# Moving SBUF tiles by 64 bytes: which half of each 128-byte line a matmul's two operands start in

## The chip, the cores and the metric

The program runs on one core of a Trainium2 chip. The metric is the device time of one execution in microseconds, 2118.91 before (median of 3 runs, 2118.55 to 2119.3). Five engines work side by side: TensorE (PE, which multiplies, with PEld as its weight loads), VectorE (DVE), ScalarE (ACT), GpSimd (POOL) and SyncE (SP, which issues most transfers). PE reads a *moving* operand (its columns stream through the array) and *weights* (a 128x128 block that a LDWEIGHTS instruction puts into the array) from SBUF, the on-chip memory, and writes PSUM.

## The reference

A two-layer encoder over 512 tokens of width 1024, float32 throughout. Per layer:

```python
h = h + 0.5 * swiglu(rmsnorm(h, g), wg, wu, wd)        # first feed-forward part, width 2816
h = h + mixer(rmsnorm(h, mix_g), ...)                  # attention; layer 0 and layer 1 differ
h = h + memory_xattn(rmsnorm(h, mg), rmsnorm(mem, sg), ...)   # attention to 256 memory rows
h = h + 0.5 * swiglu(rmsnorm(h, g), wg, wu, wd)        # second feed-forward part
# swiglu(x) = (silu(x @ wg) * (x @ wu)) @ wd
```

So there are four feed-forward parts, two mixers and two memory attentions, one after the other.

## The kernel before, in words

Activations lie transposed: eight tiles `x` of 128 features x 512 tokens. Every float32 product is done as three products of float32r parts: a tile is split into a high part (`xh`, `wh`, `hh`, a copy by ACT) and a low part (`xl`, `wl`, `hl`, what is left, by DVE), and high x high, low x high and high x low are added in PSUM.

**A feed-forward part** (`ffn`) first does one pair of 128-column blocks of gate and up with ordinary 512-column matmuls (`plain_pair`, L319). The other ten pairs are done by a scheme with seven products of half-size operands in place of eight (`open_pair`, `sum_pair`, `cross_pair`, `close_pair`). Each such product (`product`, L446) is 24 matmuls of 256 moving columns: two halves z, three pairs of parts, four blocks k. The moving operand is a quarter of the activations, either half of the tiles `xh`/`xl` or one of four combinations made once per part (`t1h`/`t1l` to `t4h`/`t4l`). The weights are a 128x1024 quarter or a sum or difference of quarters, split by `operand` into `wh`/`wl` (L424 on ACT, L425 on DVE); every third product has its split tiles `sh`/`sl` in a second pool of the feed-forward part instead. 4 parts x 10 pairs x 7 products make 280 products, 6720 matmuls. After enough pairs, `down` multiplies the hidden tiles `hh`/`hl` by the down weights in 512-column matmuls (L581), three times per part: 8, 8 and 6 hidden blocks deep, eight output blocks each.

**A mixer** weaves its projections (L683, the weights `wh`/`wl` moving, 512 columns, `xh`/`xl` as the loaded weights) with attention (L789, L814, L841, L897), the memory projection (`mem_kv`, L1080) and the output projection (`out_proj`, L634); memory attention follows (L1172 to L1230).

**Order.** PE's order is the order of the code. The order of the other engines is made at build time by a scheduler from dependencies and a cost model that knows no addresses. Places in SBUF are given by pools: a pool takes a stretch of each partition, and a tile's rotating buffers (`bufs`) lie behind one another in it, in the order in which tags first appear. Two pieces of padding in the pools `const` and `small` (PAD_CONST, PAD_SMALL, in float32) decide where what follows begins.

Of the kernel before, what the change touches and what calls it, by code (L numbers as in the profile page):

```python
# [11 lines left out]
F32 = mybir.dt.float32  # L12
F32R = mybir.dt.float32r
# [6 lines left out]
P = 128  # L20
# [39 lines left out]
WS = (2, 3, 0, 1, 1, 2, 1, 2, 0, 0, 3, 2, 1, 1, 0, 3)  # L60
FIRST = (0, 1, -1, 2, 3, -2, 4, 5, 6, -3, -4, 7)

PAD_CONST = 24
PAD_SMALL = 80

LEAD, REST = ((0, 0), (0, 1)), ((1, 0),)

# [39 lines left out]
class Encoder:  # L107
    def __init__(self, tc, ctx, I):
# [14 lines left out]
        nc.vector.memset(self.ones, 1.0)  # L123
        self.mhalf = self.const.tile([P, 8 + PAD_CONST], F32, name="mhalf")
        nc.vector.memset(self.mhalf, -0.5)
# [18 lines left out]
        return self.bank("pa" if self.pflip else "pb")  # L144

    def wtile(self):
        return [self.wp.tile([P, 1024], dt, name=n, tag=n, bufs=b) for n, dt, b in (("wf", F32, 3), ("wh", F32R, 2), ("wl", F32R, 2))]

    def behind(self, ins):

# [265 lines left out]
    def operand(self, t, own=None):  # L416

        nc, f = self.nc, self.f
        if own is None:
            own = f.n % 3 == 2  # L420
            f.n += 1
        h, l = [(f.tp if own else self.wp).tile([P, 1024], F32R, name=n, tag=n, bufs=1 if own else 2)
                for n in (("sh", "sl") if own else ("wh", "wl"))]
        self.leading = nc.scalar.activation(h, t, AF.Copy)  # L424
        self.parted = nc.vector.tensor_sub(l, t, h.bitcast(F32))  # L425
        return h, l
# [133 lines left out]
    def block(self, c, d, own=False):  # L560

        nc, f = self.nc, self.f
        n = CHUNKS[c] * P
        src = self.I[f.pre + "wd"][d, :, sum(CHUNKS[:c]) * P:sum(CHUNKS[:c]) * P + n]
        if not own:
            return self.wload(src, n), self.bank2()
        with self.tc.high_priority():
            w = self.wp.tile([P, 1024], F32, name="wf", tag="wf", bufs=3)
            h, l = [f.tp.tile([P, 1024], F32R, name=t, tag=t, bufs=1) for t in ("sh", "sl")]
            self.wfill((w, h, l), src, slice(0, n), nc.vector)  # L570
        return (h, l), self.bank2()

    def down_products(self, c, block, ops, tail):

        f = self.f
        (w, bank), nb = block, CHUNKS[c]
        for a, e in ops:
            for j in range(nb - 2, nb) if tail else range(nb - 2):
                b = sum(CHUNKS[:c]) + j
                h = f.H[b // 2][e][:, b % 2 * S:b % 2 * S + S]  # L580
                self.nc.tensor.matmul(bank, w[a][:, j * P:(j + 1) * P], h, start=j == a == e == 0,  # L581
                                      stop=j == nb - 1 and (a, e) == ops[-1])
# [420 lines left out]
    def index_keys(self, out, p, epsv, r, mp):  # L1003
# [23 lines left out]
        nc.vector.scalar_tensor_tensor(r2, r, (64 ** -0.5) * (8 ** -0.5), r, op0=OP.mult, op1=OP.mult)  # L1027
        coef = self.small.tile([P, 32 + PAD_SMALL], F32, name="coef", tag="coef", bufs=1)[:, :32]
        nc.vector.tensor_mul(coef.rearrange("p (i h) -> p i h", h=8), n3[:, :, 64:72],
# [526 lines left out]
```

## Time and profile before

| what | value |
|---|---|
| median of the runs | 2118.91 us |
| profiled execution, first to last instruction (its span) | 2114.9 us |
| PE busy in it | 2082.3 us, 98% |
| PEld busy | 1853.8 us, 88% |
| DVE busy | 1571.9 us, 74% |
| ACT busy | 1136.0 us, 54% |
| mean granted TensorE clock | 0.998 |

The profiled execution's own time is known as its span only; the median of the runs stands 4.0 us above it (what lies ahead of the first and behind the last instruction). A matmul's busy time of 280 or 390 ns overlaps that of the next, so busy times of PE don't say how fast matmuls follow one another; their starts do. The list of instructions in order of time gives these: a row is a run of like matmuls with the start of its first, so the difference of two rows' starts over the number of matmuls between is the pitch.

### The profile page before, as it was taken

Reading aid. Unit: us, or ns where it says so; the run is one execution under the profiler, and the core shown is the slowest. Engines: PE = TensorE matmul, PEld = TensorE weight load, DVE = VectorE, ACT = ScalarE, POOL = GpSimd, SP = SyncE. Lnnn points to the kernel's source line nnn. Section 1 sums busy time; section 2 is a strip of 40 time slices with the busy share of each in tenths; the row PEclk is TensorE's granted clock in tenths of the full one; section 3 lists DMA queues with packets and bytes.
Section 4 is the critical chain, followed back from the end, with each engine's and each line's share of the span. In section 5 each row is a group of like instructions: output and inputs, shape, how many; then the busy total and the mean of one; then the engine's idle time right before and its main releaser. Section 6 shows DMA issues by size and latency. Waiting matters only on the chain.

```text
span 2114.9 us, 32522 instructions
## 1 busy us (share of the span) xinstructions
PE 2082.3 (98%) x12834; PEld 1853.8 (88%) x12834; DVE 1571.9 (74%) x2246; ACT 1136.0 (54%) x1701; POOL 364.4 (17%) x319
## 2 busy tenths in 40 slices
PE   8999999999999999999999999999999999999999
PEld 7989898877788889898989899988888888989897
DVE  8858677579876697685789677684668688958676
ACT  6636344466686565362556354354678566626442
POOL 1111003345431120000020000013453122000000
PEclk9999999999999999999999999999999999999999
DMA  7836535222241266474356466334223225736532
GB/s 231 211 119 181 150 93 180 87 75 70 82 133 63 68 188 171 132 190 127 98 167 175 130 170 178 99 119 153 81 89 125 96 70 149 190 110 189 160 98 93
DMA packets 86121, 279.65 MB, mean 132 GB/s; under 512 B 9680, under 2 KB 12880, under 8 KB 85968
## 3 DMA queue, kind: packets, MB, share of 16 engines
q1 hardware_dynamic: 74448, 235.62, 33.5%
q0 software_dynamic: 11520, 41.95, 11.1%
q8 instruction: 101, 1.65, 0.3%
q14 instruction: 52, 0.43, 0.1%
HBM read 271.24 MB, written 6.29 MB: 131 GB/s over the span
## 4 chain that ended last, share of the span: by engine, by line
PE 90%; DVE 6%; ACT 2%; issue 1%; DMA 0%; POOL 0%; SPq 0%; DVEq 0%; POOLq 0%; ACTq 0%
PE ps_pa L446 26%; PE ps_pa L683 11%; PE ps_pa L581 11%; PE ps_pb L581 11%; PE ps_pb L446 10%; PE ps_pa L634 4%; PE ps_pa L319 3%; PE ps_pb L789 2%; PE ps_pa L1230 2%; PE ps_pb L841 1%; PE ps_pa L1080 1%; PE ps_pb L634 1%; PE ps_pb L814 1%; PE ps_pa L999 1%; PE ps_pb L319 1%
## 5 line engine op out<-in xcount | busy, mean ns | idle before, releaser
L157 ACT ACTIVATE wh<-wf 128x1024 fp32r<-128x1024 f32 (+2 forms) x211 | 215.5, 1022 | 353.2 <-PE ps_pa L581 119.4
L159 DVE TENSOR_TENSOR wl<-wf,wh 128x1024 fp32r<-128x1024 f32 (+2 forms) x169 | 200.3, 1188 | 49.9 <-ACT wh L157 48.0
L424 ACT ACTIVATE wh<-s 128x1024 fp32r<-128x1024 f32 x108 | 114.4, 1059 | 108.8 <-PE ps_pb L446 34.8
L425 DVE TENSOR_TENSOR wl<-s,wh 128x1024 fp32r<-128x1024 f32 x108 | 132.7, 1228 | 51.3 <-ACT wh L424 49.5
L424 ACT ACTIVATE wh<-wf 128x1024 fp32r<-128x1024 f32 x84 | 88.9, 1058 | 110.1 <-PE ps_pa L446 36.0
L503 POOL DMA_DIRECT2D s<-l_ffn_wq x40 | 35.5, 887 | 538.7 <-ACT s L502 517.0
L159 POOL TENSOR_TENSOR wl<-wf,wh 128x1024 fp32r<-128x1024 f32 x42 | 102.2, 2433 | 141.1 <-ACT wh L157 139.5
L683 PE MATMUL ps_pa<-wh,xh 128*128 128x512 f32 x384 | 123.6, 403 | 0.0
L683 PE MATMUL ps_pa<-wh,xl 128*128 128x512 f32 x384 | 120.2, 394 | 0.0
L683 PE MATMUL ps_pa<-wl,xh 128*128 128x512 f32 x384 | 119.5, 393 | 0.0
L476 POOL DMA_DIRECT2D s<-l_ffn_wq x40 | 35.6, 889 | 442.3 <-DMA s<-l_ffn_wq 314.8
L425 DVE TENSOR_TENSOR wl<-wf,wh 128x1024 fp32r<-128x1024 f32 x84 | 102.7, 1222 | 9.4 <-ACT wh L424 6.5
L591 DVE TENSOR_TENSOR dn<-ps_pa,R 128x512 f32<-128x512 f32 x48 | 33.1, 689 | 89.2 <-PE ps_pa L581 88.9
L581 PE MATMUL ps_pb<-hh,wl 128*128 128x512 f32 x352 | 96.6, 393 | 0.0
L581 PE MATMUL ps_pb<-hl,wh 128*128 128x512 f32 x352 | 96.5, 392 | 0.0
L581 PE MATMUL ps_pb<-hh,wh 128*128 128x512 f32 x352 | 96.4, 392 | 0.0
L224 POOL TENSOR_TENSOR acc<-acc,sq 128x512 f32<-128x512 f32 (+1 forms) x37 | 52.4, 1416 | 248.2 <-ACT sq L223 247.0
L581 PE MATMUL ps_pa<-hh,wl 128*128 128x512 f32 x328 | 89.7, 392 | 0.0
L581 PE MATMUL ps_pa<-hl,wh 128*128 128x512 f32 x328 | 89.5, 392 | 0.0
L581 PE MATMUL ps_pa<-hh,wh 128*128 128x512 f32 x328 | 89.5, 392 | 0.0
L591 DVE TENSOR_TENSOR dn<-ps_pb,R 128x512 f32<-128x512 f32 x48 | 33.1, 689 | 73.3 <-PE ps_pb L581 72.8
L683 PEld LDWEIGHTS ps_pa<-wh,xl 128*128 128x128 f32 x384 | 73.1, 190 | 16.2
(377 smaller groups left out, 5949.4 us busy)
## 6 DMA issues: line engine op xcount, KB each, us to landing
wf<-l_ffn_wq SPq DMA_DIRECT2D x120, 512.0 KB, 3.5
s<-l_ffn_wq SPq DMA_DIRECT2D x80, 512.0 KB, 4.6
s<-l_ffn_wq POOLq DMA_DIRECT2D x80, 512.0 KB, 6.5
wf<-l_ffn_wd SPq DMA_DIRECT2D x64, 512.0 KB, 3.7
wf<-l_w_in SPq DMA_DIRECT2D x48, 512.0 KB, 3.2
wf<-l_ffn_wd SPq DMA_DIRECT2D x32, 384.0 KB, 3.1
wf<-l_mem_wkv SPq DMA_DIRECT2D x16, 512.0 KB, 3.2
wf<-l_w_out SPq DMA_DIRECT2D x16, 512.0 KB, 3.2
```

Of the source, the lines that this page charges most:

```text
L157: self.leading = nc.scalar.activation(wh[:, sl], w[:, sl], AF.Copy)
L159: eng.tensor_sub(wl[:, sl], w[:, sl], wh.bitcast(F32)[:, sl])
L224: self.summed = (eng or nc.gpsimd).tensor_add(acc[:, :n], acc[:, :n], sq[:, :n])
L319: nc.tensor.matmul(p, w[a][:, k * P:(k + 1) * P], xs[k][c], start=k == order[0] and a == c == 0, stop=k == order[-1] and a == 1)
L424: self.leading = nc.scalar.activation(h, t, AF.Copy)
L425: self.parted = nc.vector.tensor_sub(l, t, h.bitcast(F32))
L446: self.nc.tensor.matmul(bank[:, sl], w[a][:, o:o + P], xs[k][b], start=first and z == a == b == k == 0, stop=z == a == 1 and k == KB // 2 - 1,
L581: self.nc.tensor.matmul(bank, w[a][:, j * P:(j + 1) * P], h, start=j == a == e == 0, stop=j == nb - 1 and (a, e) == ops[-1])
L591: nc.vector.tensor_mul(t, bank, f.R)
L634: nc.tensor.matmul(banks[dd], a[:, o:o + P], parts(k)[b], start=k == first and a is wh and b == 0, stop=k == last and a is wl)
L683: nc.tensor.matmul(banks[i], xs[k][a][:, i * P:(i + 1) * P], w[b][:, kk * 512:kk * 512 + 512], start=k == a == b == 0, stop=k == KB - 1 an ...
L789: nc.tensor.matmul(bank[:, o:o + n], a, b[:, :n], start=c == 0, stop=c == len(ops) - 1)
```

## The change

It moves tiles in SBUF by multiples of 64 bytes. An address bit is meant by its value: bit 6 is worth 64 bytes. All blocks that a matmul takes out of one tile begin at multiples of 512 bytes from the tile's start, so bit 6 is one for a whole tile.

- PAD_CONST and PAD_SMALL go from 24 to 40 and from 80 to 64 floats: 64 bytes more ahead, as many less behind.
- The tiles `wh`, `wl` and `sh`, `sl` get 32 floats (128 bytes) more room, so that the 1024 columns in use can begin 0 or 16 floats into them.
- `operand`, which splits the weights of the seven-product scheme, begins its columns 16 floats in (bit 6 clear), but for every sixth product (LOCK) at 0 (bit 6 set). Other users of the tiles begin at 0.

In the two programs as built, the places of the operands of the matmuls are these, in bit 6 as (moving, weights):

| matmuls | number | before | after |
|---|---|---|---|
| seven-product scheme, 256 columns | 280 products of 24 | 84 (0,0), 52 (1,1), 36 (0,1), 108 (1,0) | 236 (1,0), 44 (1,1) |
| down products, 512 columns | 2112 | 2040 (1,0), 72 (1,1) | all (1,1) |
| plain pairs, projections, queries, index, output, 512 columns | 2424 | (0,0) | (1,1) |
| memory projection, 512 columns | 192 | (0,1) | (1,1) |
| attention products in float32r | 688 | (1,1) | (1,1) |

No instruction is added, removed or moved on any engine: the two programs have the same rows in the same order with the same waits. One memset of a padded constant (`mhalf`) writes 48 in place of 32 columns.

```diff
-PAD_CONST = 24
-PAD_SMALL = 80
+PAD_CONST = 40
+PAD_SMALL = 64
+
+LINE = 16
+WIDE = 1024 + 2 * LINE
+LOCK = 6
@@ wtile
-        return [self.wp.tile([P, 1024], dt, name=n, tag=n, bufs=b) for n, dt, b in (("wf", F32, 3), ("wh", F32R, 2), ("wl", F32R, 2))]
+        return [self.wp.tile([P, c], dt, name=n, tag=n, bufs=b)
+                for n, dt, c, b in (("wf", F32, 1024, 3), ("wh", F32R, WIDE, 2), ("wl", F32R, WIDE, 2))]
@@ operand
-        h, l = [(f.tp if own else self.wp).tile([P, 1024], F32R, name=n, tag=n, bufs=1 if own else 2)
+        o = 0 if f.n % LOCK == LOCK - 1 else LINE
+        h, l = [(f.tp if own else self.wp).tile([P, WIDE], F32R, name=n, tag=n, bufs=1 if own else 2)[:, o:o + 1024]
                 for n in (("sh", "sl") if own else ("wh", "wl"))]
@@ block
-            h, l = [f.tp.tile([P, 1024], F32R, name=t, tag=t, bufs=1) for t in ("sh", "sl")]
+            h, l = [f.tp.tile([P, WIDE], F32R, name=t, tag=t, bufs=1) for t in ("sh", "sl")]
```

## The prediction

> **What bounds the kernel now.** I read the page's busy times, then the chain of work that ended last, then windows of the seven-product matmuls alone, then the list of PE's instructions in order of time. Page:
>
> ```profile
> PE 2082.3 (98%) x12834; PEld 1853.8 (88%) x12834; DVE 1571.9 (74%) x2246; ACT 1136.0 (54%) x1701; POOL 364.4 (17%) x319
> ...
> PE 90%; DVE 6%; ACT 2%; issue 1%; DMA 0%; POOL 0%; SPq 0%; DVEq 0%; POOLq 0%; ACTq 0%
> ```
>
> PE is busy nearly throughout and carries 90% of the chain, so the time moves with PE's pitch. Stretches of the seven-product scheme, L446 alone, and their sum:
>
> ```profile
> 30.00:331.00 301.00, 199.44 (x1680) 198.37 (x1680) 1.00 0.54 149
> ...
> sum 1211.00, PE 796.57 PEld 793.32; mean PE 199.14 PEld 198.33
> ```
>
> The 6720 matmuls take 796.57 us, 2.845 for each of 280 products. How long one product takes depends on its tiles. These are the first rows of ten products that follow each other without a wait (each product has six rows of four matmuls):
>
> ```profile
> 160.15 0.64 PE L446 MATMUL ps_pb<-t1h,sh 128*128 128x256 f32 x4
> ...
> 163.02 0.62 PE L446 MATMUL ps_pa<-t2h,wh 128*128 128x256 f32 x4
> ...
> 163.93 0.62 PE L446 MATMUL ps_pa<-t2h,wl 128*128 128x256 f32 x4
> ...
> 165.74 0.64 PE L446 MATMUL ps_pa<-xh,wh 128*128 128x256 f32 x4
> ...
> 168.62 0.64 PE L446 MATMUL ps_pa<-t3h,sh 128*128 128x256 f32 x4
> ...
> 171.49 0.63 PE L446 MATMUL ps_pa<-xh,wh 128*128 128x256 f32 x4
> ...
> 174.34 0.64 PE L446 MATMUL ps_pa<-t4h,wh 128*128 128x256 f32 x4
> ...
> 177.18 0.63 PE L446 MATMUL ps_pb<-xh,sh 128*128 128x256 f32 x4
> ...
> 179.91 0.62 PE L446 MATMUL ps_pb<-t1h,wh 128*128 128x256 f32 x4
> ...
> 182.63 0.62 PE L446 MATMUL ps_pa<-t2h,wh 128*128 128x256 f32 x4
> ...
> 185.35 0.64 PE L446 MATMUL ps_pa<-xh,sh 128*128 128x256 f32 x4
> ```
>
> Subtract neighbouring starts. In the built program bit 6 is set in the `t` and `sh`/`sl` tiles, clear in `xh`/`xl` and `wh`/`wl`. t1 x sh (1,1), xh x wh (0,0), t3 x sh (1,1), xh x wh (0,0) take 2.87, 2.88, 2.87, 2.85: **equal bits**, 120 ns a matmul. t2 x wh (1,0), xh x sh (0,1), t1 x wh, t2 x wh (1,0) take 2.72, 2.73, 2.72, 2.72: 113.4 ns, the **good** state. t4 x wh at 174.34 takes 2.84 though its bits differ: about 117.8 ns, the **off** state. Counting all 280 products this way I find 136 equal, 75 off, 69 good. 136x2.87 + 75x2.83 + 69x2.72 = 790.3; waits make up the other 6.3 of 796.57. So the trace of before has an effect of the very property that the change sets.
>
> What decides between good and off? In the rows above the (1,0) product after (1,1) is good (163.02), the one after (0,0) off (174.34), and good carries on from product to product (177.18 to 185.35). Over the whole trace, leaving out transitions with a wait: (1,1) to (1,0) gives good 11 times of 11, (0,0) to (1,0) off 35 of 35, good (1,0) to (1,0) stays good 11 of 11, good (1,0) to (0,1) turns off 11 of 11. A wait inside the run can throw it off: after the four transposes near a part's start the scheme is off in all four parts, here 20 matmuls in 2.35 us:
>
> ```profile
> 36.52 0.63 PE L446 MATMUL ps_pb<-t1l,wh 128*128 128x256 f32 x4
> ...
> 38.87 0.64 PE L446 MATMUL ps_pa<-t2h,sh 128*128 128x256 f32 x4
> ```
>
> **The change part by part.** *Instructions:* none is added, removed or moved on any engine, and no wait; only places change. So the sum consists of pitches of PE.
>
> *Seven-product scheme.* 236 products become (1,0), 44 (1,1): per part the products numbered 4, 10, ... 64 of 70. A (1,1) product costs 2.87 and, by 11 of 11, hands over good; then five (1,0) products follow. Bounds: all 236 good, 44x2.87 + 236x2.72 = 768.2, a gain of 22.1 against 790.3; all off, 44x2.87 + 236x2.83 = 794.2, a loss of 3.9. I take 22 off, 5 or 6 a part: products 1 to 3 behind the transposes, the two that follow the early block of the last down call (a wait there), half of product 0; the others lie behind a (1,1) product or behind (1,1) down products, which should hand over alike. 44x2.87 + 22x2.83 + 214x2.72 = 770.7: **19.6 us less**.
>
> *Down products.* 512 columns, (1,0) to (1,1). Rows with equal bits (L319, (0,0), undisturbed, then behind transposes), L581 in an 8-block call, L581 in a last call, and the few L581 with (1,1):
>
> ```profile
> 19.55 1.98 PE L319 MATMUL ps_pa<-xh,wl 128*128 128x512 f32 x8
> ...
> 26.81 0.60 PE L251 MATMUL ps_pb<-ident,acc 128*128 128x128 f32 x4
> 27.16 2.10 PE L319 MATMUL ps_pb<-xh,wh 128*128 128x512 f32 x8
> 29.10 1.99 PE L319 MATMUL ps_pb<-xl,wh 128*128 128x512 f32 x8
> 30.93 1.98 PE L319 MATMUL ps_pb<-xh,wl 128*128 128x512 f32 x8
> 32.74 0.52 PE L446 MATMUL ps_pa<-xh,wh 128*128 128x256 f32 x3
> ```
> ```profile
> 1857.45 1.54 PE L581 MATMUL ps_pa<-hh,wh 128*128 128x512 f32 x6
> ...
> 1865.69 0.62 PE L581 MATMUL ps_pa<-hh,wh 128*128 128x512 f32 x2
> ```
> ```profile
> 1412.97 1.10 PE L581 MATMUL ps_pa<-hh,wh 128*128 128x512 f32 x4
> ...
> 1429.77 0.63 PE L683 MATMUL ps_pa<-wh,xh 128*128 128x512 f32 x2
> ```
> ```profile
> 314.26 1.09 PE L581 MATMUL ps_pa<-hh,sh 128*128 128x512 f32 x4
> ...
> 317.03 0.73 PE L446 MATMUL ps_pb<-xh,wh 128*128 128x256 f32 x4
> ```
>
> Equal bits, settled: 32 matmuls in 7.26 us, 226.9. After a break they need some ten matmuls: 8 in 1.94, 8 in 1.83, 8 in 1.81. L581 (1,0): 36 in 8.24, 228.9, the same in all eight 8-block calls of 192; 72 in 16.80, 233.3, in three of the last calls. L581 (1,1), short: 12 in 2.77, 230.8. So 1536 matmuls from 228.9 to 226.8 give 3.2; some 320 at 233.3 end between 226.9 (2.1) and 230.8 (0.8), I take 1.4 as those runs are broken by waits. **4.6 less**; bounds 5.3 and, all unsettled at 230.8, a loss of 1536x1.9 - 0.8 = 2.1.
>
> *Memory projection.* (0,1) to (1,1), 192 matmuls; the nearest equal group is L683's:
>
> ```profile
> L683 PE MATMUL ps_pa<-wl,xh 128*128 128x512 f32 x384 | 119.5, 393 | 0.0
> ...
> L1080 PE MATMUL ps_pa<-wl,mh 128*128 128x512 f32 x64 | 25.6, 400 | 1.3 <-POOL wl L159 0.8 <-DVE wl L159 0.4
> ```
>
> 7 ns x 192 = 1.3 at most, nothing at least as its runs are short; I take **0.6 less**. The 2424 others go from (0,0) to (1,1), equal both times: nothing.
>
> *Cover.* A faster PE must still be fed. For the product at 163.02 DVE writes `wl` long ahead of its first use at 163.93:
>
> ```profile
> 159.88 1.23 DVE L425 TENSOR_TENSOR wl<-s,wh 128x1024 fp32r<-128x1024 f32 x1 [1.12 <-ACT wh L424]
> ```
> ```profile
> 43.00:331.00 288.00, 287.39 (x2030) 268.39 (x2029) 214.41 (x221) 137.24 (x161) 24.34 (x24) 1.00 0.53 148
> ```
>
> It ends at 161.11, 2.8 us early; five products gain 0.8 at most over the off state, and DVE is busy 214.41 of 288 us in a whole feed-forward stretch. Only the waits in a part's first products grow by what is won just ahead of them, which is next to nothing.
>
> Sum: 19.6 + 4.6 + 0.6 = 24.8. The span of 2114.9 becomes 2090.1; the median of the runs lies 4.0 above the span, so **2094**.
>
> **The rivals.**
>
> *Half good:* the state is lost at boundaries that the trace of before never had, such as good (1,0) to (1,1) and back. With half of the 236 off: 44x2.87 + 118x2.72 + 118x2.83 = 781.2, 9.1 less, with 5.2 from 512 columns 14.3: **2105**. For it: after waits the state was off more often than good. Against: 11 of 11.
>
> *Not bit 6, or not the place at all:* in before, `t` and `sh` lie in an upper region, `x` and `wh` in a lower, so in 256-column products equal bits and equal regions coincide. Were it the region, nothing changes: **2119**. Against: `hh`/`hl` lie partly in the lower region, beside `wh`, with other bit 6, and their eight calls run at 228.9 throughout, never at 226.9. [...]
>
> *All off, 512 columns as forecast:* +3.9 - 5.2: **2117.6**.
>
> *Slower: states are not reached.* Both the good state and the 226.9 are settled ones. If the new boundaries settle in neither, the scheme runs off (+3.9) and the down products at 230.8 (+2.1): +6.0, **2125**. It decides when more than nine tenths of the 236 are off and down stays unsettled; the only row for it is the short (1,1) run at 314.26.
>
> **How the numbers follow.** Forecast 0.73, half good 0.10, not bit 6 or not the place 0.08, all off 0.05, not reached 0.04. A measurement of this kernel can tell about 0.2%, 4.2 us, from no change. Faster: 0.83; same: 0.08 + 0.05 = 0.13; slower 0.04. The forecast's own range is from 2088 (all 236 good, 5.3 and 1.3: 28.7 less, 2090, and a little for a state not seen) to 2102; with the half-good case the range is 2088 to 2107, which leaves out about 2 in 10.
>
> [...]
>
> **What would show it.** L446's counterpart sums to about 777 us in its windows; products start 2.72 apart in fives behind one of 2.87; the down products' rows start 226.9 ns a matmul apart, as L319's do; L683 and waits stay. Wrong would be: fives of 2.83 (handing over fails), products still at 2.87 (not bit 6), new waits of PE on `wl` (DVE became the bound).

## The result, and the profile after

| | before | after |
|---|---|---|
| median of the runs | 2118.73 us (2118.44 to 2119.3, 4 runs) | 2106.93 us (2106.63 to 2109.09, 4 runs) |
| span of the profiled execution | 2114.9 us | 2107.3 us |
| mean granted TensorE clock | 0.998 | 0.997 |

The 2118.91 of the table ahead of the prediction is the median of the first three of these four runs. The ratio is 0.995, 95% interval 0.9935 to 0.9964: faster, by 11.8 us in the medians where 24.8 were forecast. 2106.93 lies at the upper edge of the range of 2088 to 2107. The gain of the seven-product scheme came as forecast; more than half of it was given back, in the 512-column matmuls and in new waits.

The changed file is six lines longer ahead of most of the code. L446 of before is L452 now, and so L424/L425 are L430/L431, L502 is L508, L507 is L513, L319 is L324, L581 is L587, L683 is L689, L634 is L640, L1080 is L1086. The kernels `bit7_equal`, `all_equal`, `scale_after_copy` and `copy_on_dve` of the experiments have one line more (L453, L588), and `before_bit7` has one more than before (L320, L447).

The page of after, busy times and the chain that ended last:

```profile
PE 2072.6 (98%) x12834; PEld 1837.0 (87%) x12834; DVE 1567.4 (74%) x2246; ACT 1137.1 (54%) x1701; POOL 367.1 (17%) x319
...
PE 87%; DVE 7%; ACT 3%; issue 1%; DMA 1%; POOL 0%; SPq 0%; ACTq 0%; DVEq 0%; POOLq 0%
```

PE still bounds the kernel, but 3% of the chain left it, for DVE, ACT and DMA. The busy time of the scheme's matmuls (L452) alone, summed over three windows that hold the whole span:

```profile
sum 2119.00, PE 778.98 PEld 774.62; mean PE 259.66 PEld 258.21
```

That answers the 796.57 of before; about 777 was forecast. The first row of each of seven products of after, in order of time (start, busy, engine, line, operation):

```profile
163.95 0.62 PE L452 MATMUL ps_pa<-t2h,wh 128*128 128x256 f32 x4
...
166.67 0.62 PE L452 MATMUL ps_pa<-xh,wh 128*128 128x256 f32 x4
...
169.39 0.62 PE L452 MATMUL ps_pa<-t3h,sh 128*128 128x256 f32 x4
...
172.11 0.62 PE L452 MATMUL ps_pa<-xh,wh 128*128 128x256 f32 x4
...
174.83 0.63 PE L452 MATMUL ps_pa<-t4h,wh 128*128 128x256 f32 x4
...
177.67 0.63 PE L452 MATMUL ps_pb<-xh,sh 128*128 128x256 f32 x4
...
180.41 0.62 PE L452 MATMUL ps_pb<-t1h,wh 128*128 128x256 f32 x4
```

Four products take 2.72 each, xh x wh and t3 x sh among them, which took 2.87 before. The one at 174.83, a sixth product with (1,1), takes 2.84. Now the 512-column matmuls: the first rows of successive blocks of 24 in an 8-block down call, and behind them the plain pair's rows that were shown of before from 27.16 on:

```profile
113.81 1.53 PE L587 MATMUL ps_pa<-hh,wh 128*128 128x512 f32 x6
...
119.26 1.56 PE L587 MATMUL ps_pb<-hh,wh 128*128 128x512 f32 x6
...
124.85 1.53 PE L587 MATMUL ps_pa<-hh,wh 128*128 128x512 f32 x6
...
130.31 1.56 PE L587 MATMUL ps_pb<-hh,wh 128*128 128x512 f32 x6
...
135.90 1.53 PE L587 MATMUL ps_pa<-hh,wh 128*128 128x512 f32 x6
```
```profile
26.98 2.10 PE L324 MATMUL ps_pb<-xh,wh 128*128 128x512 f32 x8
28.92 2.03 PE L324 MATMUL ps_pb<-xl,wh 128*128 128x512 f32 x8
30.79 2.03 PE L324 MATMUL ps_pb<-xh,wl 128*128 128x512 f32 x8
32.66 0.63 PE L452 MATMUL ps_pa<-xh,wh 128*128 128x256 f32 x4
```

The down blocks alternate: 5.45, 5.59, 5.46, 5.59 us for 24, so 227 and 233 ns a matmul in turn. Before they were 228.9 throughout. The plain pair's groups of eight take 1.94, 1.87, 1.87, where they took 1.94, 1.83, 1.81. Every other block uses the second of the two buffers of `wh`/`wl`. The 128 bytes that the change adds to each of these tiles put the second buffer 4224 bytes behind the first in place of 4096. 4224 is 33 times 128, so bit 7 of the address (worth 128 bytes) is now different in the second buffers. The change was described, and predicted, by bit 6 alone.

The following account adds up the starts of all matmuls in the profiled executions: the sum of the pitches of a group, and apart from it, as wait, what a pitch has above the group's usual one (where it is over 130 ns at 256 columns, 260 at 512).

| us | before | after | bit7_equal | scale_after_copy |
|---|---|---|---|---|
| scheme, pitches (6720) | 790.4 | 771.1 | 774.5 | 765.5 |
| scheme, waits | 5.3 | 10.5 | 8.2 | 5.0 |
| down products (2111) | 484.7 | 486.4 | 479.2 | 479.2 |
| projections L683 (1152) | 263.4 | 265.6 | 263.2 | 263.2 |
| output projection L634 (576) | 131.8 | 132.8 | 131.6 | 131.7 |
| plain pairs L319 (384) | 87.5 | 88.7 | 87.5 | 87.6 |
| L1230 and L999 (312) | 71.2 | 72.0 | 71.2 | 71.2 |
| memory projection L1080 (192) | 44.7 | 44.3 | 44.1 | 44.1 |
| all pitches against before | | -12.9 | -22.8 | -31.6 |
| all waits against before, other stages included | | +5.1 | +3.2 | +1.4 |

-12.9 and +5.1 are the -7.6 of the two spans but for 0.2. The waits of after, by who released PE in the scheme, and ACT's own largest:

```profile
PE ps_pa L452 <- ACT gu L513: 3.5, 4, 1.8
PE ps_pa L452 <- DVE wl L431: 2.4, 5, 0.7
```
```profile
ACT s L508 <- DMA s<-l_ffn_wq: 49.2, 34, 3.5
```

(total us, times, longest.) The same rows of before, where ACT's copy released PE in one case alone:

```profile
PE ps_pa L446 <- DVE wl L425: 1.7, 3, 0.9
...
PE ps_pa L446 <- ACT gu L507: 0.8, 1, 0.8
```
```profile
ACT s L502 <- DMA s<-l_ffn_wq: 35.1, 31, 3.4
```

The place, ACT's row first and then PE's, in after:

```profile
68.61 1.06 ACT L508 ACTIVATE s<-s 128x1024 f32<-128x1024 f32 x1 [3.14 <-DMA s<-l_ffn_wq]
69.58 1.04 ACT L430 ACTIVATE sh<-s 128x1024 fp32r<-128x1024 f32 x1
70.52 1.04 ACT L367 ACTIVATE hh<-gs 128x1024 fp32r<-128x1024 f32 x1
71.47 0.56 ACT L513 COPY gu<-ps_pa 128x512 f32<-128x512 f32 x1
```
```profile
69.67 0.62 PE L452 MATMUL ps_pa<-xh,wl 128*128 128x256 f32 x4
72.08 0.74 PE L452 MATMUL ps_pa<-t4h,wh 128*128 128x256 f32 x4 [1.79 <-ACT gu L513]
```

PE may not add t4 x wh to `pair.y` before ACT has copied it out. That copy stands in ACT's queue behind the scaling of the next pair's `s`, which waits for a DMA. PE now comes to the place sooner: its last row of xh x wl ahead of it starts at 69.67 here and at 70.20 in before. The DMA comes later: issued at 62.1, it takes 6.4 us to its landing here; issued at 62.3, 5.0 in before. In before the same two rows of ACT were

```profile
67.42 1.06 ACT L502 ACTIVATE s<-s 128x1024 f32<-128x1024 f32 x1 [1.69 <-DMA s<-l_ffn_wq]
...
70.28 0.56 ACT L507 COPY gu<-ps_pa 128x512 f32<-128x512 f32 x1
```

with an ACT that waited 1.45 us less there.

### The profile page after: what moved, and what is told of

It is laid out like the page before. It is cut to its first block, busy times and chain, and to the rows that moved or that the text cites. A ratio compares the mean times of both kernels' runs of the same rounds, so it can differ in the third digit from the quotient of the medians.

```text
span 2107.3 us, 32522 instructions
## 1 busy us (share of the span) xinstructions
PE 2072.6 (98%) x12834; PEld 1837.0 (87%) x12834; DVE 1567.4 (74%) x2246; ACT 1137.1 (54%) x1701; POOL 367.1 (17%) x319
## 4 chain that ended last, share of the span: by engine, by line
PE 87%; DVE 7%; ACT 3%; issue 1%; DMA 1%; POOL 0%; SPq 0%; ACTq 0%; DVEq 0%; POOLq 0%
PE ps_pa L452 24%; PE ps_pa L689 11%; PE ps_pa L587 11%; PE ps_pb L587 10%; PE ps_pb L452 10%; PE ps_pa L640 4%; PE ps_pa L324 3%; PE ps_pb L795 2%; PE ps_pa L1236 1%; PE ps_pb L847 1%; PE ps_pa L1086 1%; PE ps_pb L820 1%; PE ps_pb L640 1%; PE ps_pa L1005 1%; PE ps_pb L324 1%
## 5 line engine op out<-in xcount | busy, mean ns | idle before, releaser
L430 ACT ACTIVATE wh<-s 128x1024 fp32r<-128x1024 f32 x108 | 114.4, 1059 | 101.8 <-PE ps_pb L452 34.9
L431 DVE TENSOR_TENSOR wl<-s,wh 128x1024 fp32r<-128x1024 f32 x108 | 132.5, 1227 | 47.6 <-ACT wh L430 45.3
L430 ACT ACTIVATE wh<-wf 128x1024 fp32r<-128x1024 f32 x84 | 89.0, 1059 | 101.8 <-PE ps_pa L452 36.5
L689 PE MATMUL ps_pa<-wh,xh 128*128 128x512 f32 x384 | 124.2, 405 | 0.0
L689 PE MATMUL ps_pa<-wl,xh 128*128 128x512 f32 x384 | 120.5, 395 | 0.0
L689 PE MATMUL ps_pa<-wh,xl 128*128 128x512 f32 x384 | 120.5, 395 | 0.0
L431 DVE TENSOR_TENSOR wl<-wf,wh 128x1024 fp32r<-128x1024 f32 x84 | 102.6, 1221 | 7.7 <-ACT wh L430 4.6
L587 PE MATMUL ps_pb<-hh,wh 128*128 128x512 f32 x352 | 96.7, 392 | 0.0
L587 PE MATMUL ps_pb<-hl,wh 128*128 128x512 f32 x352 | 96.6, 392 | 0.0
L587 PE MATMUL ps_pb<-hh,wl 128*128 128x512 f32 x352 | 96.5, 392 | 0.0
L587 PE MATMUL ps_pa<-hl,wh 128*128 128x512 f32 x328 | 90.0, 393 | 0.0
L587 PE MATMUL ps_pa<-hh,wh 128*128 128x512 f32 x328 | 89.9, 393 | 0.0
L587 PE MATMUL ps_pa<-hh,wl 128*128 128x512 f32 x328 | 89.9, 393 | 0.0
L689 PEld LDWEIGHTS ps_pa<-wh,xl 128*128 128x128 f32 x384 | 72.8, 190 | 16.8
```

Source lines behind the costliest of these rows:

```text
L689: nc.tensor.matmul(banks[i], xs[k][a][:, i * P:(i + 1) * P], w[b][:, kk * 512:kk * 512 + 512], start=k == a == b == 0, stop=k == KB - 1 an ...
```

## The experiments

Two theories were to be tested: that bit 7 of the second buffers costs the 512-column gain, and that ACT's copy behind the scaling makes the new waits. The letters of theories are those of each expectation alone.

**Bit 7 taken away, the rest of the change kept.** The room of `wh` and `wl` becomes 1088 floats, 4352 bytes, so that second buffers differ from the first in bit 8 and not in bit 7. To make room, the tile `acc` that sums the squares of the memory rows is cut to the columns that it uses. No instruction is added, removed or moved against after.

```diff
+STRIDE = 1024 + 4 * LINE
@@ wtile
-                for n, dt, c, b in (("wf", F32, 1024, 3), ("wh", F32R, WIDE, 2), ("wl", F32R, WIDE, 2))]
+                for n, dt, c, b in (("wf", F32, 1024, 3), ("wh", F32R, STRIDE, 2), ("wl", F32R, STRIDE, 2))]
@@ square
-            acc = (pool or self.xp).tile([P, S], F32, name="acc", tag="acc", bufs=1)
+            acc = (pool or self.xp).tile([P, n if pool else S], F32, name="acc", tag="acc", bufs=1)
@@ operand
-        h, l = [(f.tp if own else self.wp).tile([P, WIDE], F32R, name=n, tag=n, bufs=1 if own else 2)[:, o:o + 1024]
+        h, l = [(f.tp if own else self.wp).tile([P, WIDE if own else STRIDE], F32R, name=n, tag=n, bufs=1 if own else 2)[:, o:o + 1024]
```

> The changed kernel with one thing altered: the tiles wh and wl get 64 more floats of room instead of 32, so that their second buffers lie 4352 bytes behind the first and not 4224 (the sum tile of the memory squares is halved to make room). With 4224 the second buffer differs from the first in address bit 7; with 4352 it does not (it differs in bit 8). In the changed kernel's trace 512-column matmuls whose operands are equal in bits 6 and 7 follow each other in 228.2 to 228.7 ns, those that differ in bit 7 in 231.9 to 232.9. Theory A (bit 7, which the extra 128 bytes flip in every second buffer, took the gain): nearly all 512-column matmuls go to about 228.4 ns; the down products from 230.4 (2111 x 2.2 = 4.6 us less), the 2424 plain, projection and output products from 230.5 (4.6 us less), the 192 of the memory projection from 231.0 (0.5 us less): 9.7 us under the changed kernel's 2106.9, so about 2097. Theory B (both bits 6 set is slower in itself than both clear): the pitches stay at 230.5 and the time at 2107. Theory C (waits that grow with a faster PE eat gains): pitches as in A, waits of PE 5 us longer, time 2102 or more.

Measured: 2097.61 us, ratio to before 0.9909 (0.9895 to 0.9923), where after has 0.995: as by A; B and C fall, as neither the pitches stayed nor the waits grew. The alternation of the down blocks is gone; first rows of blocks of 24 in the same call:

```profile
117.91 1.52 PE L588 MATMUL ps_pb<-hh,wh 128*128 128x512 f32 x6
...
123.35 1.52 PE L588 MATMUL ps_pa<-hh,wh 128*128 128x512 f32 x6
...
128.79 1.52 PE L588 MATMUL ps_pb<-hh,wh 128*128 128x512 f32 x6
...
134.23 1.52 PE L588 MATMUL ps_pa<-hh,wh 128*128 128x512 f32 x6
```

5.44 each, 226.7 ns a matmul in both buffers. Over the whole trace 512-column matmuls with bits 6 and 7 equal take 227.6 to 227.8 ns on the mean, with bit 8 equal or not. The down products stand at 479.2, 5.5 under before: the forecast's 4.6 and a little more. So bit 7 took that gain, and in these matmuls bit 8 makes no more than 0.2 ns.

The handing over from (1,1) is otherwise than in before:

```profile
170.30 0.62 PE L453 MATMUL ps_pa<-xh,wh 128*128 128x256 f32 x4
...
173.02 0.64 PE L453 MATMUL ps_pa<-t4h,wh 128*128 128x256 f32 x4
...
175.90 0.63 PE L453 MATMUL ps_pb<-xh,sh 128*128 128x256 f32 x4
...
178.69 0.62 PE L453 MATMUL ps_pb<-t1h,wh 128*128 128x256 f32 x4
...
181.41 0.62 PE L453 MATMUL ps_pa<-t2h,wh 128*128 128x256 f32 x4
```

2.72, then the (1,1) product at 2.88, then a product of 2.79 that begins off and ends good, then 2.72 again. Leaving out transitions with a wait, (1,1) hands over off 38 times of 38 here, and from off the next (1,0) product is good in 42 of 54.

**Bit 7 alone, put into the kernel before.** The rooms of `wh` and `wl` grow by 128 bytes and nothing else is changed, so second buffers lie 4224 bytes behind the first, and each tile's columns begin at the start of its room as before.

```diff
@@ wtile
-        return [self.wp.tile([P, 1024], dt, name=n, tag=n, bufs=b) for n, dt, b in (("wf", F32, 3), ("wh", F32R, 2), ("wl", F32R, 2))]
+        return [self.wp.tile([P, c], dt, name=n, tag=n, bufs=b)
+                for n, dt, c, b in (("wf", F32, 1024, 3), ("wh", F32R, 1056, 2), ("wl", F32R, 1056, 2))]
@@ operand
-        h, l = [(f.tp if own else self.wp).tile([P, 1024], F32R, name=n, tag=n, bufs=1 if own else 2)
+        h, l = [(f.tp if own else self.wp).tile([P, 1024 if own else 1056], F32R, name=n, tag=n, bufs=1 if own else 2)[:, :1024]
```

> The kernel before with one thing added: 32 floats more room for wh and wl, so that their second buffers lie 128 bytes further on; all places start as before, bit 6 of every operand stays as it was. Theory A (bit 7): the 2424 plain, projection and output products, equal in bit 6 at 228.4 ns, go to about 230.5 (half of them differ in bit 7): 5 us more; of the down products, which differ in bit 6 already, no change is known (0 to 2 us). The seven-product scheme changes by itself, as places of its weights move too: in the changed kernel equal bit 6 with other bit 7 ran at 118.9 and not 120, so it may win 2 to 8 us. Time by these 2110 to 2124; the verdict is by the lines' pitches, the plain, projection and output products above all. Theory B (both set slower than both clear): those stay at 228.4.

Measured: 2126.22 us, ratio 1.005 (1.0034 to 1.0065): slower than before. The plain pair's rows:

```profile
26.32 2.11 PE L320 MATMUL ps_pb<-xh,wh 128*128 128x512 f32 x8
28.27 2.03 PE L320 MATMUL ps_pb<-xl,wh 128*128 128x512 f32 x8
30.13 2.03 PE L320 MATMUL ps_pb<-xh,wl 128*128 128x512 f32 x8
32.00 0.63 PE L447 MATMUL ps_pa<-xh,wh 128*128 128x256 f32 x4
```

1.95, 1.86, 1.87, as in after, though bit 6 is as before, (0,0). Of the 512-column matmuls with bit 6 equal, those with bit 7 differing take 232.5 ns on the mean over the trace, those with bit 7 equal about 229. The down products lose 4.6 us, L683 2.3, L634 1.1, L319 1.2. So bit 7 is a cause by itself: it costs time where bit 6 agrees (L683, L634, L319) and where it differs (the down products). The time lies above the 2110 to 2124 expected: the down products were to lose 2 us at most, and the 2 to 8 us that the scheme was to win didn't come (its pitches sum to 791, against 790.4 in before).

**The sixth product left out.** With LOCK = 1000 all 280 products are (1,0). This is done to after alone (`no_relock`), and to bit7_equal (`bit7_equal_no_relock`).

```diff
-LOCK = 6
+LOCK = 1000
```

> The changed kernel with LOCK so large that no product of the seven-product scheme starts at offset 0: all 280 products have moving bit 6 set and weights bit 6 clear. Theory A (the relock is needed, because the good state is handed over by an equal product and an off state otherwise lasts): after the waits near a part's start and the down calls the products stay at 117.8 ns; with half of the 280 off, 140 x 2.83 + 140 x 2.72 = 777, 6 more than the 771.1 of the changed kernel: 2113. Theory B (off states end by themselves at the next product, as 13 of 15 did in the changed kernel's trace where no wait lay between): about 15 of 280 off, 265 x 2.72 + 15 x 2.82 = 763.1: 8 us less, 2099, if waits do not grow.

> Both edits: bit 7 equal by 64 floats more room for wh and wl, and no equal products in the seven-product scheme. If the two are independent, 9.7 and 8 us less than the changed kernel's 2106.9: 2089. If the off state ends by itself only because the weights' bit 7 changes from product to product (as it does with 4224 bytes between buffers and not with 4352), most products that follow a wait stay off and it is slower than the kernel with bit 7 equal and equal products kept: 2097 plus 6, 2103.

Measured: 2102.99 us, 0.9935 (0.9923 to 0.9948), and 2091.67 us, 0.988 (0.9867 to 0.9894), 4 and 3 us above the 2099 and 2089 expected if off ends by itself. The scheme's pitches fall to 765.2 and 766.7 from after's 771.1 and bit7_equal's 774.5; 248 and 228 of the 280 products are good. Without a wait, good stays good in 198 of 203 transitions of no_relock, and off turns good again in 8 of 9; in the other kernel 174 of 183 and 18 of 32. Where the following product has no wait inside it either, no good one turned off in these two traces. So the off state ends by itself here, at the next product or at a later one, and each sixth product costs its 0.15 us and often some of the next product for nothing.

**All products (1,1).** bit7_equal with its LOCK changed.

```diff
-LOCK = 6
+LOCK = 1
```

> bit7_equal with every product of the seven-product scheme at bit 6 set in both operands: 280 (1,1) in place of 236 (1,0) and 44 (1,1); 512-column matmuls as in bit7_equal, bits 6 and 7 equal. Theory A (the difference of bit 6 between moving operand and weights sets the pitch of 256-column products): all 280 take 2.875 us, the scheme's pitches sum to 805, 30.5 more than in bit7_equal (774.5), and as PE is slower the waits fall from 8.2 to about 5: 2097.6 + 27.3 = 2125, slower than before although the 512-column matmuls stay at 227.6 ns. Rival B (the gain in bit7_equal comes from what the weights' tiles start at or from the room between them, and not from bit 6 against the moving operand): products at 2.72 to 2.80, about 2098.

Measured: 2123.77 us, 1.0035 (1.0023 to 1.0046). All 280 products are equal in bit 6 and take 2.87 each on the mean, without waits. The scheme's busy time over the whole span,

```profile
sum 2119.00, PE 808.83 PEld 806.35; mean PE 269.61 PEld 268.78
```

against 782.56 in bit7_equal; the 512-column matmuls are as there. The 64 bytes turn bit 7 of the weights as well as bit 6, so this pair of runs doesn't part the two bits; after's trace does. There, among products with bit 7 equal in all their matmuls and no wait, 50 (1,0) ones are good and take 2.72, four are off at 2.82, and the nine (1,1) ones take 2.875. Two parts of the change are so priced apart: the scheme's 256-column places are worth 26 us (2123.77 against 2097.61, on two chips), and the 512-column ones some 6.5 (5.5 in the down products, 0.6 in the memory projection, 0.4 in the rest of the account).

**The order on ACT.** The scaling of `s` may no longer be placed ahead of the previous pair's copy; places as in bit7_equal_no_relock, which ran again beside it. And, apart from it, that copy done by DVE.

```diff
-        nc.scalar.copy(c, self.halves(pair.y))
+        f.copied = nc.scalar.copy(c, self.halves(pair.y))
...
-            with self.behind(f.led):
+            with self.behind(f.led), self.behind(getattr(f, "copied", None)):
                 nc.scalar.activation(s, s, AF.Copy, scale=-1.0)
```
```diff
-        nc.scalar.copy(c, self.halves(pair.y))
+        nc.vector.tensor_copy(c, self.halves(pair.y))
```

> bit7_equal_no_relock with one more order on ACT: the scaling of a pair's `s` (which waits for its DMA) may not be placed ahead of the copy out of `pair.y` in cross_pair of the pair before. Places in SBUF as in bit7_equal_no_relock, the same work; the order of some rows of ACT, DVE and POOL shifts with it. Theory C (the added waits of the faster scheme come from that copy standing behind the scaling and its DMA): the waits of the products at the end of each pair's crossing product, 3.0 us of 9.1 in bit7_equal_no_relock, go, the copy releases PE no more, scheme waits about 6: 2 to 3 us less than bit7_equal_no_relock, 2089. Rival D (the copy is only the last of several suppliers that are late): PE waits at the same places or the next ones for `wl` or for the later scaled `s`, scheme waits 9 or more, 2091 to 2094.

> bit7_equal_no_relock with that copy out of `pair.y` done by DVE, ahead of DVE's addition of `pair.z` to it, in place of ACT: 40 copies of about 0.56 us leave ACT's queue and go to DVE's. Theory C: ACT no longer releases PE at that place, scheme waits fall by up to 3.0 us if DVE is free there: 2089. Rival D, or DVE's own queue (it also makes `wl`) being late: waits on `wl` or on DVE's copy take their place, scheme waits 9 or more, 2091 to 2095.

> bit7_equal_no_relock again, on the same chip as the two that change its waits, to compare them with: 2091.7 as measured, within 2; scheme waits 9, of which ACT's copy releases 2.0 and DVE's `wl` 2.6.

| | median us | ratio to before | scheme waits us |
|---|---|---|---|
| bit7_equal_no_relock_2 | 2092.31 | 0.9885 (0.9868 to 0.9901) | 11.4 |
| scale_after_copy | 2086.47 | 0.9859 (0.9845 to 0.9874) | 5.0 |
| copy_on_dve | 2096.47 | 0.9908 (0.9893 to 0.9923) | 12.6 |

The same place in scale_after_copy, ACT and PE:

```profile
69.77 0.57 ACT L514 COPY gu<-ps_pa 128x512 f32<-128x512 f32 x1
70.23 1.07 ACT L509 ACTIVATE s<-s 128x1024 f32<-128x1024 f32 x1
```
```profile
70.33 0.62 PE L453 MATMUL ps_pa<-xh,wl 128*128 128x256 f32 x4
70.78 0.62 PE L453 MATMUL ps_pa<-t4h,wh 128*128 128x256 f32 x4
```

The copy ends at 70.34, 0.44 us before t4 x wh begins, and PE passes without a wait. ACT's waits for the DMA of `s` are gone as well, first bit7_equal_no_relock_2, then scale_after_copy:

```profile
ACT s L509 <- DMA s<-l_ffn_wq: 47.6, 36, 3.1
```
```profile
ACT s L509 <- DMA s<-l_ffn_wq: 1.8, 2, 1.1
```

The waits at the ends of the crossing products, with the first matmul behind each, are gone: 4.5 us in one profile of the kernel without the order, 6.4 in the other. The median falls by 5.8 us, more than the 2 to 3 expected: these waits vary from execution to execution (the scheme's are 9.1 and 11.4 in the two profiles), and fewer breaks leave more products good, 239 in place of 228. The scheduler places other rows of ACT, DVE and POOL anew with this order, so it is not the only thing that moved. The copy on DVE is no gain but a loss of 4.2 us: ACT's copy releases PE no more, but DVE's does, and DVE falls behind elsewhere (the waits of the down products on PE rise from 3.1 to 6.8 us). It is the place in the queue that has to be changed, and DVE's is no better (copy_on_dve):

```profile
PE ps_pa L453 <- DVE wl L432: 2.7, 3, 1.2
PE ps_pa L453 <- DVE gu L514: 2.2, 3, 1.0
PE ps_pb L453 <- DVE gu L515: 1.0, 1, 1.0
PE ps_pb L453 <- ACT sq L229: 0.9, 1, 0.9
```

**The same order in the changed kernel and in the kernel before.**

> The changed kernel with the order of scale_after_copy alone added (places as in the changed kernel). Theory C: the waits of the crossing products that ACT's copy releases, 5.7 us of the scheme's 10.5 (products 13, 20, 27, 34, 41 and 48 of a part, with the first matmul of the next), go: scheme waits about 5, 2106.9 - 5.5 = 2101.5. Rival D (another supplier is as late in the changed kernel): 2105 or more. The 512-column pitches stay at 228.7 and 232.3 to 232.9.

> The kernel before with the same order alone. Theory C (ACT's copy becomes late only when the scheme is faster): of its 5.3 us of waits 1.6 lie at those places, so at most 1.6 less, about 2116 where the kernel before is at 2117.5; the order is no gain of its own. Rival E (the order is worth its 5 us whatever the places): 2112.

Measured: 2101.56 us, 0.9927 (0.9914 to 0.9939), with scheme waits of 4.9 for after's 10.5; and 2115.39 us, 0.9993 (0.9984 to 1.0002), with 3.9 for 5.3. So the order is worth some 5 us only where the scheme is fast: that copy became late with the change.

scale_after_copy, at 2086.47 us, is the fastest of all; it is 1.4% under before and 0.9% under after by the ratios.

## Why the prediction was right or wrong

**The span and what lies around it: mis-sized.** The prediction set 4.0 us around the span. Where the time of the profiled execution is known beside its span, the difference is 1.8 or 1.9 (2109.09 and 2107.3 in after, 2101.3 and 2099.4 in after_order). So the profile of before came, by estimate, from an execution of about 2116.7, 2 us under its median, and after's from one 2 us over its own. The spans therefore differ by 7.6 and the medians by 11.8; the account by pitches and waits is of the former.

**Seven-product scheme, "19.6 us less": right in size, in part by luck.** The pitches fell by 19.3. Bit 6 is what sets them in the main: 2.72 against 2.875 with bit 7 equal, in one trace; and xh x wh, which keeps its region, takes 2.72 where it took 2.87. Two details behind the number were off and nearly cancel. Of the 236 products 204 are good and 32 off (214 and 22 forecast). Of the 44 priced at 2.87 most take 2.84: by places, the 27 without a wait whose bit 7 differs take 2.844 on the mean, the 9 whose bit 7 is equal 2.875. One reading was wrong, though no term hangs on it: 796.57 is busy time, so waits can't "make up the other 6.3" of it; by starts the pitches are 790.4 and the waits 5.3 beside them.

**"By 11 of 11, hands over good": wrong as a rule.** In bit7_equal the same (1,1) to (1,0) hands over off 38 of 38. What the 11 had in common besides bit 6 is that bit 7 was equal in all of them; in bit7_equal it differs, wholly or in part, in every (1,0) product, since 64 bytes more behind a place with bit 6 set carry into bit 7. After's trace shows that this alone doesn't decide: there, without a wait, the (1,0) product behind a (1,1) one differs in bit 7 each time, and it was good 26 times of 26 where the (1,1) product differs in bit 7 too, and off 8 times of 9 where that one agrees. Why is open. So what carried the term is partly that 33 of the 44 (1,1) products happen to differ in bit 7, which the prediction did not look at, and partly a thing that it did not have: off ends by itself, in after at the next (1,0) product in 13 cases of 13 without a wait. The sixth products, which it took as the price of staying good, are a loss of 4 to 6 us in the medians (after to no_relock, bit7_equal to bit7_equal_no_relock); the intervals of the first pair overlap, but the scheme's pitches fell by 5.9 and 7.8.

**Down products, "4.6 us less": wrong sign, +1.7.** The rows with equal bits from which 226.9 was taken had bit 7 equal too. With that kept, bit7_equal measures 5.5 less, so the term was right for the property named and not for the places that the change makes.

**"The 2424 others go from (0,0) to (1,1), equal both times: nothing": this step failed.** L683, L634, L319, L1230 and L999 lost 5.2 us together, in their second buffers. The step looked at one address bit of where a tile begins, and took no account of how far apart the buffers of a tile now lie. Down and these make 11.5 of what was missing.

**Cover, "next to nothing": wrong, 5.1 us of waits.** This step failed too. The row shown for cover was DVE's `wl`, and it held: DVE releases PE for 2.4 us, 1.7 before. What ended last was ACT's copy out of `pair.y` behind a scaling that waits for a DMA, in a queue for which no row was read. after_order, which asks for another order there and keeps the places, takes the scheme's waits from 10.5 to 4.9.

So of 24.8, the missing parts in the profiled executions are 6.3 (down), 5.2 (others), 5.1 (waits), 0.3 (scheme) and 0.2 (memory projection, 0.4 in place of 0.6): 7.7 is left, and the spans show 7.6.

**The rivals.** Half good (2105) has the time nearly right and the mechanism wrong: 204 of 236 were good. All off and not reached fall with that count. In *not bit 6, or not the place at all* (2119), that no place matters was shown by no run: in before already, equal work took 2.87 and 2.72 by its tiles. The condition that "down stays unsettled" came near, but the 233 ns of after is no unsettled state: it stays through 24 matmuls, ends with the buffer, and returns with it. What made the 233.3 in three of before's last calls, with bit 7 equal, stays open.

## What to carry to other kernels

When a tile is padded to move its start, look at where all of its rotating buffers come to lie: the start of the second one is set by the tile's size, and here that cost as much as half of the gain of the first: from after to bit7_equal, where the second buffers' bit 7 agrees again, the pitches fall by 9.9 us, and the scheme's gain was 19.3. Price a placement with a kernel that changes one address bit at a time, before a rule is built on the bits that happen to differ. And when a stage becomes faster, read the queue of every engine that must release it, above all for an instruction that waits for a DMA ahead of the one that releases: here PE's waits for such a copy went from 0.8 to 3.5 us.

## What the runs showed of the hardware

- 512-column float32r matmuls, where the moving operand and the weights agree in bits 6 and 7: 226.7 ns in the down blocks of bit7_equal, and on the mean 227.6 to 229.3 over the traces of before, after, bit7_equal and before_bit7, with those just behind a break or another buffer counted and attention left out. Where they agree in bit 6 and differ in bit 7: 232.5 to 232.8 on the mean. With bit 6 differing and bit 7 equal: 228.9 in the 8-block calls of before, but 233.3 in three of its last calls. With both differing: 232.6 to 232.8 in before_bit7. Bit 8 makes no difference in bit7_equal (means within 0.2 ns).
- 256-column ones: 119.5 to 120 ns with both bits equal, 118.5 in after with bit 6 equal and bit 7 differing, 113.4 with bit 6 differing in the good state, with bit 7 equal or not.
- Where the scheme's weights begin makes 26 us here: bit7_equal and all_equal have the same instructions in the same order and take 2097.61 and 2123.77 us (on two chips), with the weights of 236 of the 280 products beginning 64 bytes apart. Why, no run shows.
- What decides between good and off at a boundary stays open. In no_relock good turned off in 15 of 44 transitions with a wait. Without a wait, off turned good at the next product 8 times of 9 there; in before it stayed off 13 times of 13 from (0,1) to (1,0) and turned good 19 times of 19 from (1,0) to (0,1).
